# Between two layers: the residual rows requested two blocks ahead, and the low parts of the normed rows moved from GpSimd to VectorE

## The chip, the cores and the metric

The kernel runs on one core of a Trainium2 chip. A core has TensorE (PE in the profile; its weight loads are a row of their own, PEld), VectorE (DVE), ScalarE (ACT), GpSimd (POOL) and SyncE (SP), which issues almost all DMAs here. The metric is the device time of one execution in microseconds; lower is better. Three runs of the kernel before took 1369.54, 1370.9 and 1371.71 us.

## The reference, cut to what matters

The reference is one inference step of a two-layer encoder: 512 prompt rows and 32 sample rows of width 1024. Each layer is `x + (branch * silu(gate)) @ w_out`, with the branch made from `rmsnorm(x) @ w_in`. Layer 0 mixes tokens by RWKV-7, layer 1 by differential attention; both also attend to 256 memory rows, whose keys and values are `rmsnorm(mem) @ w_mem_k` and `@ w_mem_v`. The part at issue is where layer 0 ends and layer 1 begins:

```
x1  = x + out @ w_out[0]                       # residual add of layer 0
h   = x1 * rsqrt(mean(x1*x1) + EPS) * norm_w[1]
mk, mv = rmsnorm(mem) @ w_mem_k[1], rmsnorm(mem) @ w_mem_v[1]
p   = h @ df_in                                # input projection of layer 1
```

## The kernel before, in words

All activations are held transposed: 1024 features are eight tiles of 128 partitions (`KT = 8`), and the 544 tokens (512 + 32) lie along the free axis. Every float32 product is made of three products of rounded numbers. An operand is split into a high part, rounded to fp32r, and a low part, the rest, so `w @ x` is `whi*xh + whi*xl + wlo*xh`. For weights, `raw` arrives by DMA, ScalarE casts it to `whi`, VectorE subtracts to get `wlo` (helper `split`, two halves of 128x512 each). For activations the pair is called `hi`/`lo` in layer 0's output projection, `hh`/`hl` as the normed input of a layer, and `mmh`/`mml` for the memory rows.

One helper records every instruction of TensorE, VectorE, ScalarE and SyncE, so the profile gives them all line 106, and they are told apart by tile names. Up to the end of the output projection the order of each engine's instructions is written out by hand (`self.ordered = True`). After `self.ordered = False` (line 1745) the recording layer chooses the order on each engine by itself. Whatever the source, an engine or a DMA queue works its instructions off in order: one that waits holds all behind it. A DMA on SP also waits until the DMA eight before it (roughly: the one that used the same of eight completion counters) has landed.

The stages around the change, in order of time:

- *The last head pair of layer 0 and the start of its output projection.* The 16 gated outputs lie in a scratch tensor in HBM, `oscr`. Five are fetched and split ahead; the other eleven are fetched in `w_out` (SP: `lo<-oscr`, 272 KB each; then ScalarE `hi<-lo`, VectorE `lo<-lo,hi`).
- *The output projection* `w_out(0, ...)`, with eight output blocks k of 128 features. For each block, `residual` turns the 32x32 pieces of the residual rows `xr` to feature-major on VectorE (`x<-xr`, a stream transpose of 128x544), and `consume` adds TensorE's sums to them and squares them on ScalarE (`sqn`) for the norm (`sums`).
- *`rows(k)`* asks for the residual rows of block k: four DMAs of 64 KB from `x_prompt`, in pieces of 32 numbers, and four of 4 KB from `x_sample`. It is called once ahead (`rows(0)`, line 1717, before `w_out` asks for anything), and then for block k+1 from `residual` of block k.
- *Between the layers* (line 1747 on): the mean of squares by small products (`ps_n`), a reciprocal root of eight small VectorE instructions (`tm_...`), five diagonal tiles `dg` by which TensorE spreads the roots over the partitions (`ps_r`), and the loop over k, lines 1757 to 1764: `hn` (VectorE, 128x512 and 128x32), `hh` (ScalarE cast), `hl = hn - hh` (GpSimd, line 1763). TensorE meanwhile makes the memory keys and values of layer 1 (`mem_kv`: eight blocks of 24 products of 256 columns, `ps_g<-mmh,...`; `memx`, `memz`, `memt` and `ps_mkt` carry its results out), and then starts layer 1's projection with `ps_g<-hh,whi`, `ps_g<-hl,whi`, `ps_g<-hh,wlo`.

The constants are `HNB = 3` (buffers of `hn`) and `RAWS = 5` (buffers of raw weights).

Of the kernel before, what the change touches and what calls it, by code (L numbers as in the profile page):

```python
# [9 lines left out]
F32 = mybir.dt.float32  # L10
# [4 lines left out]
ALU = mybir.AluOpType  # L15
AX = mybir.AxisListType

P = 128
# [4 lines left out]
T = TP + TS  # L23
# [16 lines left out]
HNB = 3  # L40
# [68 lines left out]
class Trunk:  # L109
# [1330 lines left out]
    def layer0(self, mem):  # L1440
        nc, o = self.nc, self.o
# [5 lines left out]
        with ExitStack() as ctx:  # L1447
# [23 lines left out]
            def go(kind, pr):  # L1471

                if kind == "rsq":
                    self.rsqrt(self.r20[:], self.q20[:], self.rk0, "nt")
                elif 0 <= pr < NPAIR:
                    if kind in ("inv", "back", "at"):
                        {"inv": self.rw_invert, "back": self.rw_back, "at": self.rw_at}[kind](sts[pr])
                        return
                    if (kind, pr) not in run:
                        it = run[kind, pr] = self.rw_prep(sts[pr], rkv[pr]) if kind == "prep" else make[kind](sts[pr])  # L1480
                        next(it)
                    next(run[kind, pr], None)
# [203 lines left out]
        with ExitStack() as ctx:  # L1686
            p = self.pool("wo0", 1, ctx=ctx)
            sums = p.tile([P, T], F32, name="sums")
            xs, again = [], self.mem_again(mh, ml)

            def rows(k):

                if k < KT:
                    x = p.tile([P, T], F32, tag="xr", name="xr", bufs=2)
                    for a in range(4):
                        r, f = slice(TS * a, TS * a + TS), slice(k * P + TS * a, k * P + TS * a + TS)
                        self.se.dma_start(x[r, :TP].rearrange("i (b c) -> i b c", c=TS),
                                          self.a["x_prompt"][0, :, f].rearrange("(b i) c -> i b c", i=TS))
                    for a in range(4):
                        r, f = slice(TS * a, TS * a + TS), slice(k * P + TS * a, k * P + TS * a + TS)  # L1700
                        self.se.dma_start(x[r, TP:], self.a["x_sample"][0, :, f])
                    xs.append(x)

            def residual(k, vs):

                if vs[0].start == 0:
                    rows(k + 1)
                    self.ve.transpose(self.x1[:, k, :], xs[k][:])

            def consume(k, ps, v):  # L1710
                x = self.x1[:, k, v]
                self.ve.tensor_tensor(x, ps, x, ALU.add)
                self.square_sums((k, x, v), p, sums)
                if k > 1:
                    next(again, None)

            rows(0)
            self.ahead = after[2:] + [(self.a[n][1], h * P) for n in ("w_mem_k", "w_mem_v") for h in range(MH)] + self.blocks1()
            wout, ahead = self.w_out(0, p, OUT_ORDER, consume, residual, made)

            def both():
                yield from main
                for _ in range(2):
                    self.early.append(self.load(*self.ahead.pop(0)))
                self.until(self.last_split)
                yield from wout
            both = both()

            def fill2(n):
                for i in range(n):  # L1730
                    next(both, None)
                    if i % 6 == 5:
                        self.some(LATER)

            for kind, n in TAIL:
                if kind == "split":
                    ahead(1)
                else:
                    go(kind, NPAIR - 1)
                fill2(n)  # L1740
            for _ in both:
                pass
            while self.later:
                self.later.pop(0)[0]()
            self.ordered = False

            rs = self.token_rms((sums,), p)
            kv = chain(*(self.mem_kv(1, mh, ml, kind, self.psm, "m") for kind in range(2)))
            next(kv)
            pr = [self.psc.tile([P, 512], F32, tag="c", name="ps_r") for _ in range(2)]  # L1750
            for i in range(5):
                n = P if i < 4 else TS
                dg = p.tile([P, P], F32, tag="dg", name="dg", bufs=2)
                self.ve.tensor_scalar(dg[:], self.ident[:], rs[:, i : i + 1], None, ALU.mult)
                c = i % 4 * P
                self.te.matmul(pr[i // 4][:, c : c + n], self.ones[:], dg[:, P - n :], start=True, stop=True)
            for k in range(KT):
                h = p.tile([P, T], F32, tag="hn", name="hn", bufs=HNB)
                for q, c, n in ((0, 0, TP), (1, TP, TS)):
                    self.ve.scalar_tensor_tensor(h[:, c : c + n], self.x1[:, k, c : c + n], self.nw[1][:, k : k + 1],  # L1760
                                                   pr[q][:, :n], ALU.mult, ALU.mult)
                self.ae.copy(self.hh[:, k, :], h[:])
                nc.gpsimd.tensor_tensor(self.hl[:, k, :], h[:], self.hh[:, k, :].bitcast(F32), ALU.subtract)  # L1763
                next(kv, None)
            for _ in kv:
                pass
# [479 lines left out]
```

## Time and profile before

| what | value |
|---|---|
| runs | 1369.54, 1370.9, 1371.71 us |
| the profiled execution | 1371.42 us |
| its span, first to last instruction | 1369.2 us |
| TensorE busy in the span | 1339.3 us (98%), weight loads 1283.9 us (94%) |
| VectorE, ScalarE, GpSimd busy | 939.7, 822.6, 381.9 us |
| granted TensorE clock, mean | 0.998 |

Numbers of a trace are microseconds from the start of the span. A row of a timeline gives start, length, engine, line, operation, tiles, count, and in brackets how long the engine stood idle before it and what ended that. A length of several instructions is from the start of the first to the end of the last; neighbours overlap by a little, since the next starts before the last one's results are all written. Because TensorE carries the span almost alone, the places where its weight loads stand still are what a change can win or lose.

### The profile page before, as it was taken

What the parts mean: (1) busy time and instruction counts of PE and PEld (TensorE: products, weight loads), DVE (VectorE), ACT (ScalarE), POOL (GpSimd) and SP (SyncE); (2) the same over time, 40 slices, a digit from 0 to 9 for tenths busy, and PEclk for the clock granted to TensorE, in tenths of its full rate; (3) what the DMA queues carried; (4) which work ended last, traced back from release to release, by engine and by line L of the source; (5) the groups of instructions that cost most, each with busy time, mean ns of one, the idle gap of its engine ahead of it and who ended that gap; (6) DMA issues with size and microseconds to landing.
All of it is one profiled execution on the core that took longest, in us unless ns stands there. A gap on an engine that the chain in (4) does not pass through costs nothing. (4 is left out here: it accounts for less than half of the span.)

```text
span 1369.2 us, 31861 instructions
## 1 busy us (share of the span) xinstructions
PE 1339.3 (98%) x11845; PEld 1283.9 (94%) x11845; DVE 939.7 (69%) x2353; ACT 822.6 (60%) x2288; POOL 381.9 (28%) x841
## 2 busy tenths in 40 slices
PE   8999999999999999999999999999999999999997
PEld 6988899999999998988999989999999999999997
DVE  5776788888888888667744667775567747667443
ACT  5766777877778777656433466654566537665222
POOL 2138667766686667600000120000000001002000
PEclk9999999999999999999999999999999999999999
DMA  7452322333323332432555563332333323332322
GB/s 224 146 140 70 77 71 57 94 86 74 88 67 84 88 88 64 142 87 76 173 142 147 148 184 88 100 102 82 101 95 94 90 82 94 97 97 79 93 78 73
DMA packets 276964, 139.06 MB, mean 102 GB/s; under 512 B 75769, under 2 KB 265730, under 8 KB 276810
## 3 DMA queue, kind: packets, MB, share of 16 engines
q1 hardware_dynamic: 276746, 137.01, 36.0%
q8 instruction: 94, 1.54, 0.5%
q14 instruction: 60, 0.49, 0.1%
q10 hardware_dynamic: 64, 0.02, 0.0%
HBM read 110.72 MB, written 22.91 MB: 98 GB/s over the span
## 5 line engine op out<-in xcount | busy, mean ns | idle before, releaser
L106 PE MATMUL ps_g<-hh,whi 128*128 128x272 f32 x1808 | 539.7, 299 | 1.0 <-DVE ats L106 0.7
L106 PE MATMUL ps_g<-hh,wlo 128*128 128x272 f32 x1808 | 534.8, 297 | 1.6 <-DVE wlo L106 1.5
L106 PE MATMUL ps_g<-hl,whi 128*128 128x272 f32 x1808 | 532.4, 295 | 0.6 <-DVE hl L106 0.3
L106 PEld LDWEIGHTS ps_g<-hh,whi 128*128 128x128 f32 x1808 | 341.2, 189 | 5.1 <-DVE ats L106 0.9
L106 PEld LDWEIGHTS ps_g<-hh,wlo 128*128 128x128 f32 x1808 | 340.6, 189 | 4.7 <-DVE wlo L106 2.5
L106 PEld LDWEIGHTS ps_g<-hl,whi 128*128 128x128 f32 x1808 | 341.1, 189 | 2.8 <-DVE hl L106 1.3
L106 DVE TENSOR_TENSOR wlo<-raw,whi 128x512 fp32r<-128x512 f32 x314 | 220.1, 712 | 118.3 <-ACT whi L106 114.7
L106 ACT CAST whi<-raw 128x512 fp32r<-128x512 f32 x314 | 188.9, 619 | 115.8 <-PE ps_g L106 62.4
L868 POOL TENSOR_TENSOR tm<-u,m 102x84 f32<-102x84 f32 (+23 forms) x341 | 147.8, 433 | 115.4 <-DMA m<-sc 69.5
L870 POOL TENSOR_TENSOR u<-u,tm 102x84 f32<-102x84 f32 (+23 forms) x341 | 151.6, 445 | 26.6
L106 PE MATMUL ps_g<-hi,wlo 128*128 128x272 f32 x512 | 147.8, 289 | 1.2 <-DVE wlo L106 1.2
L106 PE MATMUL ps_g<-hi,whi 128*128 128x272 f32 x512 | 147.7, 289 | 0.0
L106 PE MATMUL ps_g<-lo,whi 128*128 128x272 f32 x512 | 147.4, 288 | 0.0
L1339 POOL TENSOR_TENSOR lo<-og,hi 128x544 fp32r<-128x544 f32 x8 | 13.2, 1649 | 357.7 <-ACT hi L106 357.2
L106 PEld LDWEIGHTS ps_g<-hi,wlo 128*128 128x128 f32 x512 | 96.4, 188 | 1.7 <-DVE wlo L106 1.6
L106 PEld LDWEIGHTS ps_g<-hi,whi 128*128 128x128 f32 x512 | 96.5, 189 | 0.0
L106 PEld LDWEIGHTS ps_g<-lo,whi 128*128 128x128 f32 x512 | 96.4, 188 | 0.0
L106 ACT ACTIVATE pt<-ps_s,snm 128x128 f32<-128x128 f32 (+3 forms) x96 | 51.0, 532 | 41.7 <-DVE snm L106 41.6
L1763 POOL TENSOR_TENSOR hl<-hn,hh 128x544 fp32r<-128x544 f32 x8 | 12.2, 1536 | 211.4 <-ACT hh L106 211.3
L106 DVE SCALAR_TENSOR_TENSOR SB<-ps_c,dl,sd 64x64 f32<-64x64 f32 x168 | 47.4, 282 | 26.4 <-PE ps_c L106 21.2
L106 ACT COPY sv<-ps_c 64x64 f32<-64x64 f32 x192 | 39.6, 206 | 32.7 <-PE ps_c L106 30.8
L106 ACT ACTIVATE sg<-ps_g 128x272 f32<-128x272 f32 x64 | 25.2, 394 | 41.0 <-PE ps_g L106 38.3
(400 smaller groups left out, 2564.4 us busy)
## 6 DMA issues: line engine op xcount, KB each, us to landing
raw<-in_rw_in_dram SPq DMA_DIRECT2D x114, 256.0 KB
raw<-in_df_in_dram SPq DMA_DIRECT2D x112, 256.0 KB
raw<-in_w_out_dram SPq DMA_DIRECT2D x64, 256.0 KB
oscr<-sg SPq DMA_DIRECT2D x16, 272.0 KB
lo<-oscr SPq DMA_DIRECT2D x16, 272.0 KB
m<-sc SPq DMA_DIRECT2D x33, 128.0 KB
raw<-in_w_mem_v_dram SPq DMA_DIRECT2D x16, 256.0 KB
kh<-kh SPq DMA_DIRECT2D x24, 136.0 KB
```

The costliest lines, as they stand in the source:

```text
L106: return lambda *a, **k: self.trunk.tie(self, issue(*a, **k))
L868: nc.gpsimd.tensor_tensor(tm[:, :n, :wd], u3[:, :n, kx : kx + 1].to_broadcast(sh), m3[:, kx : kx + 1, kx + 1 :].to_broadcast(sh), ALU.mult)
L870: nc.gpsimd.tensor_tensor(u3[:, :n, kx + 1 :], u3[:, :n, kx + 1 :], tm[:, :n, :wd], ALU.add)
L1339: (self.nc.gpsimd if g % 2 and self.o1 else self.ve).tensor_tensor(lo[:], t, hi[:].bitcast(F32), ALU.subtract)
L1763: nc.gpsimd.tensor_tensor(self.hl[:, k, :], h[:], self.hh[:, k, :].bitcast(F32), ALU.subtract)
```

## The change

The residual rows take buffers under the tag `hn` instead of their own two, so rows and normed rows share three buffers. The rows of block k+2 instead of k+1 are asked for in block k, with `rows(0)` and `rows(1)` both called ahead. The subtraction `hl` goes from GpSimd to VectorE.

```diff
-                    x = p.tile([P, T], F32, tag="xr", name="xr", bufs=2)
+                    x = p.tile([P, T], F32, tag="hn", name="xr", bufs=HNB)
...
                 if vs[0].start == 0:
-                    rows(k + 1)
+                    rows(k + 2)
                     self.ve.transpose(self.x1[:, k, :], xs[k][:])
...
             rows(0)
+            rows(1)
...
                 self.ae.copy(self.hh[:, k, :], h[:])
-                nc.gpsimd.tensor_tensor(self.hl[:, k, :], h[:], self.hh[:, k, :].bitcast(F32), ALU.subtract)
+                self.ve.tensor_tensor(self.hl[:, k, :], h[:], self.hh[:, k, :].bitcast(F32), ALU.subtract)
```

What this does to the order of instructions shows at three places. The first is SP's queue where layer 0's output projection begins; `xr` are residual rows, `lo5` to `lo8` gated outputs, `raw` weights. Before:

```order
L106 DMA oscr1_476<-sg2_83 128x544
L106 DMA xr_10584<-in_x_prompt_dram 32x16x32 x4
L106 DMA xr_10584<-in_x_sample_dram 32x32 x4
L106 DMA lo5_10594<-oscr0_475 128x544
L106 DMA lo6_10597<-oscr0_475 128x544
```

Now, from the same place on:

```order
L106 DMA xr_10584<-in_x_prompt_dram 32x16x32 x4
L106 DMA xr_10584<-in_x_sample_dram 32x32 x4
L106 DMA xr_10593<-in_x_prompt_dram 32x16x32 x4
L106 DMA xr_10593<-in_x_sample_dram 32x32 x4
L106 DMA lo5_10603<-oscr0_475 128x544
L106 DMA lo6_10606<-oscr0_475 128x544
```

Eight more DMAs, the rows of block 1, stand ahead of all eleven fetches of gated outputs and of the weights behind them. The last group of eight, which stood between the first weights of `w_mem_k`, is gone from there.

The second place is VectorE at the end of the output projection, where the sums of squares (`sums`) are finished and the root (`tm_m`) begins; `wlo` are low parts of the memory weights:

```order
 L106 TENSOR_TENSOR x_10579<-ps_g,x_10579 128x272
-L106 TENSOR_TENSOR wlo<-raw,whi 128x512
-L106 TENSOR_TENSOR sums<-sums,sqn 128x272
-L106 TENSOR_TENSOR wlo<-raw,whi 128x512
+L106 TENSOR_TENSOR sums<-sums,sqn 128x272
 L106 TENSOR_SCALAR tm_m_11850<-ps_n 128x5
+L106 TENSOR_TENSOR wlo<-raw,whi 128x512
```

The sums now come straight after the last residual add, ahead of both `wlo`. ScalarE's last `sqn` has likewise moved ahead of three `whi`.

The third is VectorE in the loop over k; eight rows of before, from the second `hn` on:

```order
L106 SCALAR_TENSOR_TENSOR hn<-x_10579,PB,ps_r 128x512
L106 SCALAR_TENSOR_TENSOR hn<-x_10579,PB,ps_r 128x32
L106 TENSOR_TENSOR wlo<-raw,whi 128x512
L106 SCALAR_TENSOR_TENSOR hn<-x_10579,PB,ps_r 128x512
L106 SCALAR_TENSOR_TENSOR hn<-x_10579,PB,ps_r 128x32
L106 TENSOR_TENSOR wlo<-raw,whi 128x512
L106 TENSOR_TENSOR memz<-memx,mo 128x256
L106 TENSOR_TENSOR wlo<-raw,whi 128x512
```

Now:

```order
L106 SCALAR_TENSOR_TENSOR hn<-x_10579,PB,ps_r 128x512
L106 SCALAR_TENSOR_TENSOR hn<-x_10579,PB,ps_r 128x32
L106 TENSOR_TENSOR hl<-hn,hh 128x544
L106 TENSOR_TENSOR wlo<-raw,whi 128x512
L106 TENSOR_TENSOR hl<-hn,hh 128x544
L106 TENSOR_TENSOR wlo<-raw,whi 128x512
L106 TENSOR_TENSOR memz<-memx,mo 128x256
L106 SCALAR_TENSOR_TENSOR hn<-x_10579,PB,ps_r 128x512
```

The eight `hl` are spread between the `wlo` and `hn` of VectorE's queue, each waiting for ScalarE's `hh` of the same k. The last `hl` stands behind all eight `hn` and ahead of the `wlo` of layer 1's third weight block.

## The prediction

> **What bounds the kernel now.** I read the page first, then the waits of the weight loads in two stretches, then the queues that those waits point to.
>
> ```profile
> PE 1339.3 (98%) x11845; PEld 1283.9 (94%) x11845; DVE 939.7 (69%) x2353; ACT 822.6 (60%) x2288; POOL 381.9 (28%) x841
> PE 42%; DVE 1%; ACT 0%; issue 0%; DVEq 0%; ACTq 0%
> L1763 POOL TENSOR_TENSOR hl<-hn,hh 128x544 fp32r<-128x544 f32 x8 | 12.2, 1536 | 211.4 <-ACT hh L106 211.3
> ```
>
> TensorE carries the span and the last chain. So only places count where its weight loads stand still. From the fetch of the outputs to the last residual add (664 to 764) the waits of PEld are one row:
>
> ```profile
> PEld ps_g L106 <- DVE wlo L106: 1.0, 1, 1.0
> ```
>
> Between the layers (764 to 800) they are five:
>
> ```profile
> PEld ps_g L106 <- DVE wlo L106: 2.2, 3, 1.2
> PEld ps_mkt L106 <- ACT memx L106: 1.5, 4, 0.6
> PEld ps_r L106 <- DVE dg L106: 0.6, 2, 0.4
> PEld ps_n L106 <- DVE sums L106: 0.4, 1, 0.4
> PEld ps_g L106 <- ACT whi L106: 0.3, 1, 0.3
> ```
>
> They add to 5.0 us: that is all the change can win there. In the first stretch it can win at most 1.0, and lose.
>
> **The change part by part: the rows two blocks ahead.** What was late? The transposes of VectorE are the only readers of `xr`; their group shows the idle time ahead of them in the last column:
>
> ```profile
> L106 DVE STREAM_TRANSPOSE x<-xr 128x544 f32<-128x544 f32 x8 | 5.9, 738 | 0.0
> ```
>
> It is 0.0 for all eight: no row was ever waited for, so asking earlier wins 0. The group of eight DMAs taken from the end of the projection frees SP of 4 us there, also for 0, since PEld waits for nothing between its one wait at 681.6 and 764. The third buffer costs 0 too: by the time `hn` takes it, its rows have been transposed.
>
> The price is at the start. SP's queue before:
>
> ```profile
> 663.36 2.08 SPq L106 DMA_DIRECT2D xr<-in_x_prompt_dram  x4
> 665.49 1.88 SPq L106 DMA_DIRECT2D xr<-in_x_sample_dram  x4
> 667.47 1.79 SPq L106 DMA_DIRECT2D lo<-oscr  x4
> 669.36 3.21 SPq L106 DMA_DIRECT2D raw<-in_w_out_dram  x4
> 672.62 3.34 SPq L106 DMA_DIRECT2D lo<-oscr  x5
> ...
> 684.46 3.41 SPq L106 DMA_DIRECT2D xr<-in_x_prompt_dram  x4
> 687.91 3.35 SPq L106 DMA_DIRECT2D xr<-in_x_sample_dram  x4
> ```
>
> Eight row DMAs take 667.47 - 663.36 = 4.1 us of SP. A second group now stands between the first and `lo`, so the `lo` start at about 671.6. Who waits for them is seen on ScalarE:
>
> ```profile
> 672.06 2.79 ACT L106 CAST hi<-lo 128x544 fp32r<-128x544 f32 x4 [2.77 <-DMA lo<-oscr]
> 678.20 0.65 ACT L106 CAST hi<-lo 128x544 fp32r<-128x544 f32 x1 [3.34 <-DMA lo<-oscr]
> 679.09 0.65 ACT L106 CAST hi<-lo 128x544 fp32r<-128x544 f32 x1 [0.24 <-DMA lo<-oscr]
> 679.64 1.14 ACT L106 CAST whi<-raw 128x512 fp32r<-128x512 f32 x2
> ```
>
> and on the weight loads:
>
> ```profile
> 681.59 0.19 PEld L106 LDWEIGHTS ps_g<-hi,wlo 128*128 128x128 f32 x1 [0.98 <-DVE wlo L106]
> ```
>
> The `whi` at 679.64 is queued behind casts that waited for `lo9` and `lo10`; its `wlo` is what TensorE waited 0.98 us for. That chain has no slack: what delays `lo10` delays TensorE as much. Does `lo10` come 4.1 us later? The windows:
>
> ```profile
> core 0: us, PE busy (x) PEld busy (x) DVE busy (x) ACT busy (x) POOL busy (x), PEclk, DMA share, GB/s
> 664.00:668.00 4.00, 4.00 (x34) 4.00 (x33) 3.61 (x9) 1.27 (x3) 0.00 (x0) 1.00 0.61 122
> 669.00:679.00 10.00, 10.00 (x82) 9.91 (x81) 6.18 (x12) 3.53 (x6) 0.00 (x0) 1.00 0.99 330
> 764.00:800.00 36.00, 33.18 (x260) 30.87 (x259) 29.82 (x56) 21.00 (x49) 13.30 (x12) 1.00 0.54 157
> ```
>
> From 669 to 679 the DMA engines are busy 0.99 of the time: nine `lo` and four `raw` are moved as fast as they go, so the train shifts as a whole, by the 4.1 us. TensorE stalls in two bites of the same shift (first at `lo5`, used about 1.6 us after it was ready, so 4.1 - 1.6 = 2.5; the rest at the `wlo`). Nothing later gives it back: all behind it follows TensorE. Bounds: 0 at the low end, if the casts had slack that I do not see (their 2.77 and 3.34 us of waiting speak against that); at the high end 3.41 + 3.35 = 6.8 us, what the same eight DMAs took at 684.46. I take 4.1, the nearer row: same place in the queue, same neighbours. **Term 1: +4.1 us.**
>
> The Trainium skill, "DMA: Bandwidth & Descriptors", in the table of measured transfers under Bandwidth, gives 0.95 us of DMA time for 64 KB and 0.68 us for 4 KB (measured from GpSimd's queue). By that a group of rows is 4 x 0.95 + 4 x 0.68 = 6.5 us, an estimate, and the sum would be 2.4 us higher. The trace does not agree: from 664 to 668, while SP issued rows, the DMA engines were busy only 0.61 of the time, so issue set the pace and not transfer.
>
> **The low parts on VectorE.** While GpSimd works on `hl`, VectorE's subtractions stretch. In the window 779.5 to 799 of its groups (after the bar: busy us, mean ns of one, idle time ahead):
>
> ```profile
> L106 DVE TENSOR_TENSOR wlo<-raw,whi 128x512 fp32r<-128x512 f32 x10 | 11.5, 1176 | 1.2 <-ACT whi L106 1.2
> L106 DVE TENSOR_TENSOR memz<-memx,mo 128x256 f32<-128x256 f32 x2 | 2.6, 1287 | 0.0
> ```
>
> and from 764 to 779.5, with GpSimd idle:
>
> ```profile
> L106 DVE TENSOR_TENSOR wlo<-raw,whi 128x512 fp32r<-128x512 f32 x7 | 4.7, 689 | 3.9 <-ACT whi L106 3.9
> L106 DVE TENSOR_TENSOR memz<-memx,mo 128x256 f32<-128x256 f32 x2 | 0.8, 421 | 0.0
> ```
>
> The stretch is 10 x (1.176 - 0.689) + 2 x (1.287 - 0.421) = 4.9 + 1.7 = 6.6 us of VectorE, all in the stage where PEld waits for `wlo`. It goes. What comes is eight subtractions of 128x544; such instructions stand in the trace:
>
> ```profile
> 682.05 1.35 DVE L106 TENSOR_TENSOR lo<-lo,hi 128x544 fp32r<-128x544 f32 x2
> 683.33 1.28 DVE L106 TENSOR_TENSOR wlo<-raw,whi 128x512 fp32r<-128x512 f32 x2
> ...
> 772.33 0.17 DVE L106 TENSOR_SCALAR tm_m<-ps_n 128x5 f32<-128x5 f32 x1 [0.32 <-PE ps_n L106]
> ...
> 777.90 1.72 DVE L106 SCALAR_TENSOR_TENSOR hn<-x,PB,ps_r 128x512 f32<-128x512 f32 x4
> 779.53 0.68 DVE L106 TENSOR_TENSOR wlo<-raw,whi 128x512 fp32r<-128x512 f32 x1
> ```
>
> Two `lo` take 683.33 - 682.05 = 1.28 us, 0.64 each, so eight `hl` 5.1 us: VectorE's load falls by 1.5 us. But now they wait in line. I laid the new order out with these lengths. The sums stand ahead of two `wlo`, so `tm_m` starts at about 769.9 instead of 772.3, and the first `hn` at about 775.7 instead of 777.9. From there to the last `hl` VectorE has 8 `hn` pairs of (779.53 - 777.90) / 2 = 0.82, 8 `hl` of 0.64, 12 `wlo` of 0.62 and 3 `memz` of 0.35: 6.5 + 5.1 + 7.4 + 1.1 = 20.1 us, so 795.8, and 1.0 for waits on ScalarE's `hh`: about 796.8. GpSimd ended its last at 797.48 + 1.35 = 798.8:
>
> ```profile
> 797.48 1.35 POOL L1763 TENSOR_TENSOR hl<-hn,hh 128x544 fp32r<-128x544 f32 x1 [1.01 <-ACT hh L106]
> ```
>
> TensorE's waits then: for `wlo` 2.2 to 0 and for `whi` 0.3 to 0 (made in time without the stretch), for `sums` 0.4 to 0, for `memx` 1.5 to 0.3 (ScalarE's copies no longer bunch behind late `hh`), for `dg` 0.6 to 0.9 (TensorE arrives earlier), and new, for the last `hh` and `hl`, 1.1, since without the other stalls it reaches them at 795.7. That is 2.3 against 5.0. **Term 2: -2.7 us.** Bounds: -5.0, all waits gone; and +1, if the queue ends its last `hl` a microsecond after GpSimd did. I take what the layout gives, nearer to the first, since VectorE's load falls. GpSimd's two sets of clears for layer 1, which came after its last `hl`, now run some 35 us earlier and are waited for by nobody.
>
> **Sum.** +4.1 - 2.7 = +1.4 us on the profiled execution of 1371.4 (span 1369.2 and 2.2 around it), which lies 0.5 above the median of the three runs, 1370.9. Against that median: 1372.3 us, +0.1%, below the 0.2% (2.7 us) that a measurement of this kernel tells from no change.
>
> **The rivals.**
> - *Slower: VectorE's queue becomes the new wait.* One `hl` whose `hh` is late holds the `wlo` and `hn` behind it, and TensorE waits for `wlo` as before. Decides from where the last `hl` ends after 798.8, so with 2 us more of waits than I laid out. Then term 2 is 0, and the time 1370.9 + 4.1 = 1375.0. For it: ScalarE casts `whi` in the same queue. Against: 6.6 us of stretch go. Chance 0.16.
> - *Slower: the second rows cost the 6.8 us of 684.46:* 1370.9 + 6.8 - 2.7 = 1375.0. For it: pieces of 32 numbers are slow to move. Against: the share of 0.61. Chance 0.05.
> - *Faster: the `lo` train is hidden.* If the casts' wait were shortened elsewhere, term 1 is under 1 and the time near 1370.9 - 2.7 = 1368.2. Against: 0.99 of DMA share and the 0.98 us stall. Chance 0.12.
> - *All 5.0 us between the layers go*, term 1 holds: 1370.0; no difference that can be told. That lies inside the forecast's case, as does the part of the change that does nothing, the rows that nobody waited for.
>
> **How the numbers follow.** Forecast 0.67 (1369 to 1373.6), the slower rivals 0.21, the faster 0.12. With the edges, where a forecast in its own range can cross the bound: faster 0.13, same 0.64, slower 0.23. The range for 8 in 10 goes from the faster rival's 1368.2 to the slower ones' 1375.0, each widened by 0.5, by which the profiled execution and the median differ: 1367.7 to 1375.5.
>
> **What would show it.** In the profile after: sixteen `xr` DMAs on SP ahead of `lo`, `lo` at about 671.6, the first `hi` cast at about 676; PEld waiting about 5 us instead of 1.0 between 664 and 764, for `lo`, `hi` or `wlo`; `wlo` at 0.69 us throughout; `hl` on VectorE ending 2 us sooner relative to the last residual add than before; PEld's waits between the layers near 2.3. Wrong would be: no new wait near 675 to 686 (term 1), or waits for `wlo` and `hl` between the layers still above 4 (term 2).

## The result: 0.18% slower

| kernel | median | runs | ratio to before, 95% interval |
|---|---|---|---|
| before | 1370.65 us | 22 (1369.14 to 1372.45) | |
| changed | 1373.41 us | 22 (1371.47 to 1374.77) | 1.0018 (1.0012 to 1.0025) |

The change costs 2.8 us by the medians and 0.18% by the ratio, which is a figure of its own and not the quotient of the medians: clear of zero, and at the edge of the 0.2% (2.7 us) that the forecast called no change. The forecast was 1372.3 us. The profiled execution has a span of 1371.5 us, 2.3 more than before:

```profile
span 1371.5 us, 31837 instructions
PE 1340.3 (98%) x11845; PEld 1285.4 (94%) x11845; DVE 937.7 (68%) x2361; ACT 822.1 (60%) x2288; POOL 368.1 (27%) x833
```

Both traces hold 11,845 weight loads, and outside the stretch from 765 to 803, where TensorE's order changed too, they come in the same order. So the start of the n-th load in one can be set against the start of the n-th in the other. That lateness, the measure used from here on, is 0.0 us at 660, +5.8 at 700 and 764, +2.1 at 812, and +2.4 near the end. So the gated outputs' stretch lost 5.8 us, and the stage between the layers won 3.7 back; the rest adds 0.3.

**The loss.** The queue of SP after, from its first row DMA on:

```profile
663.35 2.08 SPq L106 DMA_DIRECT2D xr<-in_x_prompt_dram  x4
665.47 1.88 SPq L106 DMA_DIRECT2D xr<-in_x_sample_dram  x4
667.39 2.02 SPq L106 DMA_DIRECT2D xr<-in_x_prompt_dram  x4
669.45 2.41 SPq L106 DMA_DIRECT2D xr<-in_x_sample_dram  x4
671.96 1.79 SPq L106 DMA_DIRECT2D lo<-oscr  x4
```

The first `lo` is asked for at 671.96, where it was 667.47. The waits of the weight loads from 664 to 764, one row of 1.0 us before, are now:

```profile
PEld ps_g L106 <- ACT whi L106: 1.9, 1, 1.9
PEld ps_g L106 <- DVE lo L106: 1.1, 2, 0.6
PEld ps_g L106 <- DVE wlo L106: 1.1, 1, 1.1
PEld ps_g L106 <- ACT hi L106: 1.1, 2, 0.7
```

They add to 5.2 us, 4.2 more than before. The lateness grew by 5.8. The missing 1.6 us stands in the windows just ahead of and behind 685.7, in the column after the busy times (PEclk):

```profile
682.30:685.70 3.40, 1.16 (x8) 0.73 (x6) 2.25 (x4) 2.88 (x6) 0.00 (x0) 1.00 0.52 188
685.70:689.10 3.40, 3.00 (x13) 3.00 (x14) 3.40 (x7) 2.25 (x5) 0.00 (x0) 0.50 0.93 276
```

TensorE worked for 1.16 of 3.40 us, and then the granted clock was 0.50 for the next 3.4 us: 13 products where the same stretch of before held 30. At half clock, 3.4 us of work lose 1.7.

**The gain.** From 764 to 812 the waits were 5.0 us before; after they are 1.7:

```profile
PEld ps_mkt L106 <- ACT memx L106: 0.7, 2, 0.6
PEld ps_g L106 <- ACT hh L106: 0.7, 1, 0.7
PEld ps_r L106 <- DVE dg L106: 0.3, 1, 0.3
```

VectorE's subtractions from 779.5 to 803 (after the bar: busy us, mean ns of one) are back at the length that they had with GpSimd idle, 685 ns instead of 1176, and `hl` costs 717 ns each, 5.7 us for the eight:

```profile
L106 DVE TENSOR_TENSOR wlo<-raw,whi 128x512 fp32r<-128x512 f32 x14 | 9.4, 685 | 0.4 <-ACT whi L106 0.2
L106 DVE TENSOR_TENSOR hl<-hn,hh 128x544 fp32r<-128x544 f32 x8 | 5.7, 717 | 1.2 <-ACT hh L106 1.2
```

### The profile page after: what moved, and what is told of

The parts are those of the page before. It is cut to its first block, busy times and chain, and to the rows that moved or that the text cites. A ratio compares the mean times of both kernels' runs of the same rounds, so it can differ in the third digit from the quotient of the medians.

```text
span 1371.5 us, 31837 instructions
## 1 busy us (share of the span) xinstructions
PE 1340.3 (98%) x11845; PEld 1285.4 (94%) x11845; DVE 937.7 (68%) x2361; ACT 822.1 (60%) x2288; POOL 368.1 (27%) x833
## 4 chain that ended last, share of the span: by engine, by line
PE 87%; ACT 4%; DVE 4%; DMA 2%; issue 1%; SPq 1%; POOL 1%; DVEq 0%; ACTq 0%; POOLq 0%
PE ps_g L106 61%; PE ps_c L106 6%; PE ps_s L106 2%; PE ps_o L106 2%; PE ps_at L106 2%; PE ps_v L106 2%; PE ps_mm L106 1%; SPq L106 1%; PE ps_w L106 1%; PE ps_mo L106 1%; PE ps_aT L106 1%; PE ps_yc L106 1%; PE ps_wa L106 1%; PE ps_kv L106 1%; PE ps_q L106 1%
## 5 line engine op out<-in xcount | busy, mean ns | idle before, releaser
L106 DVE TENSOR_TENSOR wlo<-raw,whi 128x512 fp32r<-128x512 f32 x314 | 215.5, 696 | 114.9 <-ACT whi L106 111.3
```

The source lines that it names most:

```text
L106: return lambda *a, **k: self.trunk.tie(self, issue(*a, **k))
```

## The experiments

Each kernel's median stands beside that of the kernel before in the same set of runs; before itself moved between the sets, so kernels of different sets are compared by their ratios. For the order at the seam alone the medians and the ratio do not even agree in sign: there the runs show no difference. The last three columns are changes of TensorE's lateness in the profiled execution: in the gated outputs' stretch (660 to 700), between the layers (764 to 812), and over the whole from 660 to the end. They are of one execution each. The six kernels whose first stretch has no rows added ahead and none taken away show -0.2 to +0.5 there, and the seven with rows two ahead, low parts on VectorE and GpSimd not subtracting show -3.4 to -3.9 between the layers; a difference between two rows as small as that says nothing by itself.

| kernel | median, before | ratio, 95% interval | 660-700 | 764-812 | total |
|---|---|---|---|---|---|
| changed | 1373.41, 1370.65 | 1.0018 (1.0012 to 1.0025) | +5.8 | -3.7 | +2.4 |
| rows part alone | 1376.91, 1371.67 | 1.0035 (1.0023 to 1.0048) | +7.8 | -1.6 | +6.1 |
| low parts alone | 1369.49, 1371.67 | 0.9985 (0.9976 to 0.9994) | +0.2 | -2.7 | -2.0 |
| both, second rows late | 1367.93, 1371.67 | 0.9974 (0.9963 to 0.9985) | 0.0 | -3.8 | -3.5 |
| low parts, first rows late | 1368.22, 1371.67 | 0.9977 (0.9967 to 0.9987) | +0.1 | -2.8 | -2.6 |
| both, half of the second rows ahead | 1372.66, 1371.39 | 1.0007 (0.9998 to 1.0016) | +4.7 | -3.6 | +1.4 |
| second rows late, GpSimd subtracts too | 1374.37, 1371.39 | 1.0022 (1.0012 to 1.0032) | +0.5 | +2.4 | +2.9 |
| both, three groups ahead | 1376.82, 1371.39 | 1.0041 (1.0027 to 1.0054) | +8.2 | -3.8 | +4.7 |
| order at the seam alone | 1370.84, 1371.39 | 1.0002 (0.9993 to 1.0010) | -0.1 | -1.3 | -1.0 |
| changed, TensorE's wait filled | 1373.46, 1372.01 | 1.0011 (1.0002 to 1.0019) | +4.5 | -3.7 | +1.2 |
| order and low parts | 1368.81, 1372.01 | 0.9976 (0.9965 to 0.9986) | +0.2 | -3.8 | -3.2 |
| second rows late, GpSimd clears | 1368.69, 1372.01 | 0.9975 (0.9965 to 0.9985) | -0.2 | -3.9 | -3.6 |
| both, all rows late | 1367.34, 1372.01 | 0.9967 (0.9955 to 0.9978) | -1.1 | -3.4 | -4.1 |

### The two parts, one at a time

The rows part alone (from the changed kernel):

```diff
-                self.ve.tensor_tensor(self.hl[:, k, :], ...
+                nc.gpsimd.tensor_tensor(self.hl[:, k, :], ...
```

> The row part of the change alone: rows two blocks ahead in the shared buffers, the low parts still on GpSimd. Theory A (the second group of rows ahead of the gated outputs delays TensorE, the stretch of VectorE by GpSimd is untouched): PEld waits between 664 and 764 near 5.2 us as in the changed kernel, TensorE 5.9 us late at 700, wlo between the layers still near 1.18 us, time 1370.65 + 5.9 = 1376.5 us. Rival B (the gain between the layers came with the rows, whose last group of DMAs left the end of the projection): TensorE's waits from 764 to 803 fall from 5.0 to about 1.7 here too, and the time is that of the changed kernel, 1373.4 us. Rival C (the half clock after the wait is the luck of one execution): 1370.65 + 4.2 = 1374.8 us.

The low parts alone (from the kernel before):

```diff
-                nc.gpsimd.tensor_tensor(self.hl[:, k, :], ...
+                self.ve.tensor_tensor(self.hl[:, k, :], ...
```

> The VectorE part of the change alone: the eight low parts on VectorE, rows as before (one block ahead, two buffers of their own). Theory A: no new wait from 664 to 764 (1.0 us), wlo near 0.69 us between the layers, PEld's waits from 764 to 812 about 1.7 us instead of 5.0, time 1370.65 - 3.7 = 1367.0 us. Rival B (that gain came with the rows): about 1370.6 us. Rival D (without the earlier delay, which let the weights and ScalarE get ahead of TensorE, the queue of VectorE is tighter): about half the gain, 1368.8 us.

The rows part alone loses 7.8 us in the first stretch (its waits there are 6.0 us, and its half clock lasted two of the 3.4 us pieces), but it also wins 1.6 us between the layers, though GpSimd still stretches the subtractions:

```profile
L106 DVE TENSOR_TENSOR wlo<-raw,whi 128x512 fp32r<-128x512 f32 x12 | 12.6, 1062 | 1.2 <-ACT whi L106 1.2
```

Up to the end of the output projection this kernel is the changed one; that it lost 7.8 us there and the changed one 5.8 is a difference between two executions, in how long the half clock lasted. The runs (1.0035) lie between theory A (1.0043) and rival C (1.0030), and their interval holds both; rival B (1.0020) lies outside.

The low parts alone win 2.7 us there, not 3.7. So theory A had the first stretch right, and each theory had a part of the second: the gain between the layers has two sources, 1.0 to 1.6 us of it from the rows. Rival D forecast about half the gain, and the size came near it (2.1 us by the ratio), but not for its reason: in the next kernel nothing is delayed earlier, and 3.8 us are won.

### Where in the queue the rows stand

Both parts, with the second group behind the gated outputs:

```diff
             rows(0)
-            rows(1)
...
                 if vs[0].start == 0:
+                    if k == 0:
+                        rows(1)
                     rows(k + 2)
```

> The whole change, but the second group of rows is asked for together with the third in the first block's residual, behind the gated outputs. Theory A: the place in the queue is all that costs, so the same as with the low parts alone, 1367.0 us, and no half clock. Rival E (two groups of rows in a row on the queue at 684 hold the weights behind them for another 4 to 7 us, and TensorE waits there): a new wait for whi or wlo near 695 to 705, 1368 to 1371 us.

The low parts, rows one block ahead, and the first group asked for after gated output 14:

```diff
-            rows(0)
...
                 came.append((g, self.fetch(p, g)))
+                if i == 0 and g == 14:
+                    extra(-1, None)      # residual(-1, ...) calls rows(0)
```

> The low parts on VectorE, rows one block ahead, and the first group of rows asked for behind the gated output 14 instead of ahead of 5: 4.1 us less of the queue ahead of the gated outputs. Theory A (that train has no slack): the wait of 1.0 us at 681.6 goes and nothing more, since TensorE waits for nothing else up to 764: 1366.0 us. Rival F (the train is held by what comes earlier, the write of the gated outputs, so it starts no sooner): 1367.0 us. Rival E (the rows, now at 673 to 680 between large transfers, land late for their transpose at 688, or hold the later gated outputs): a wait for x or hi near 685, 1367 to 1369 us.

With the second group late, the loss in the first stretch is gone (0.0) and the gain of 3.8 stays: 0.26% faster than before, theory A's time, so the place of eight DMAs is the whole loss of the change. Moving the first group as well, with the low parts alone, took away the wait at 681.6 and put one of 1.1 us behind the last gated outputs at 689, as rival E had it in kind; theory A's 1366.0 us (0.9966) lies just outside the interval:

```profile
689.21 0.19 PEld L106 LDWEIGHTS ps_g<-hi,whi 128*128 128x128 f32 x1 [0.49 <-ACT hi L106]
689.97 0.19 PEld L106 LDWEIGHTS ps_g<-lo,whi 128*128 128x128 f32 x1 [0.57 <-DVE lo L106]
```

Both edits together, on the kernel with both parts:

```diff
-            rows(0)
-            rows(1)
...                                          # rows(0) behind gated output 14
+                    if k == 0:
+                        rows(1)
```

> The kernel with the second group of rows late, and the first group behind the gated output 14 as well. Theory A (the wait of 1 us at 681.6 only moves on to the last gated outputs, as it did with the low parts alone): within 0.5 us of the kernel with the rows late, 3.6 us below before. Rival Q (the two gains add): 0.7 to 1 us more, 4.5 us below before.

Here the weight loads wait for nothing from 664 to 764. It is the best version measured: 0.33% below before. The first stretch wins 1.1 us, as rival Q had it; against the kernel with only the second group late it is 0.6 us better over the whole trace and 1.0 by the ratios. The intervals overlap, so the last microsecond is not settled by the runs. Why the wait at 689 stayed away here and not in the other kernel is not shown. Both have the same order on SP up to there, and SP reached the write of the last gated outputs at 679.99 here and at 681.10 there, so it may be no more than a difference between two executions.

How the loss grows with what stands ahead, half of the second group:

```diff
-            rows(1)
+            rows(1, prompt only)     # the sample rows of block 1 come in residual(0)
```

> The changed kernel with only half of the second group of rows (the four DMAs from the prompt) ahead of the gated outputs, its other four behind them. Theory A (the delay is the issue time that stands ahead, 2.1 us for four): PEld's waits from 664 to 764 near 1.0 + 2.1 = 3.1 us instead of 5.2, and by that less idle no stretch at half clock: 2.1 us above the kernel with the group behind (1367.9), 1370.0 us. Rival C (any such wait brings 3.4 us at half clock, which cost 1.7): 1371.7 us. Rival G (the pieces of 4 KB from the sample rows are what holds the queue): no new wait, 1368 us.

And a third group (the first block's `residual` then asks for none):

```diff
             rows(1)
+            rows(2)
```

> The changed kernel with a third group of rows (block 2) ahead of the gated outputs. Theory A (every eight row DMAs shift the whole train by 4.1 us, and TensorE by as much): PEld's waits from 664 to 764 near 9.3 us, the stretch at half clock one or two windows of 3.4 us (1.7 us of loss each, one of them in the changed kernel already): 1373.4 + 4.1 = 1377.5 to 1379.2 us. Rival I (the first 4.1 us filled a hole and further rows are limited by their transfers, of 6 us or more): 1380 us or more. Rival B (the train's start is set elsewhere and the wait stays): 1373.4 us.

Four DMAs more give waits of 3.1 us, as theory A had them (1.0 + 2.1):

```profile
PEld ps_g L106 <- ACT whi L106: 2.0, 1, 2.0
PEld ps_g L106 <- DVE wlo L106: 1.1, 1, 1.1
```

But a half clock followed here too, for 6.8 us, and the loss was 4.7, so rival C is nearest. In these two executions half of the group costs nearly as much as the whole; by the ratios (1.0007 and 1.0018) it costs 1.5 us less. The third group is cheaper than theory A or rival I said: +8.2 in the first stretch instead of 9.9 to 11.6, and by the ratios 3.2 us above the changed kernel instead of 4.1 to 5.8. Its waits are 7.4 us, most of them in one piece,

```profile
681.01 0.29 PEld L106 LDWEIGHTS ps_g<-hi,whi 128*128 128x128 f32 x1 [4.87 <-ACT hi L106]
```

and the half clock (678.7 to 685.5) began while TensorE still stood in that wait. Measured against the lateness at 660, the first cast of `whi` behind the train came 3.8 us later than in the changed kernel (688.90 - 684.01 - 1.1), so the train shifted nearly as before. That the slow clock used up some of the later waiting fits this and is not shown by itself.

### The half clock

In all these traces the pieces of half clock between 600 and 810 are 3.41 us or twice that, and in one trace their starts lie whole multiples of 3.4133 us apart (131.33, 800.35 and 1366.96 in the kernel where GpSimd subtracts too: 196 and 166 of them), as on a grid. Where the clock fell, the weight loads had been busy for 0.7 to 1.4 us of the piece of this grid before; between 600 and 810 no piece at full clock with 1.7 us or more was followed by a fall. To see whether standing still is the cause, 14 products with a zero weight tile were put just where TensorE stood still for 1.95 us (they add zero to sums in progress):

```diff
+                if i == 0 and (k, q) == (0, 1) and gs[0] == half[1][0]:
+                    for n in range(14):
+                        v = halves[n % 2]
+                        self.te.matmul(ps[0][v.start // TH][:, :TH], zero[:], o[half[0][0]][0][:, v], start=False, stop=False)
```

> The changed kernel with 14 products of a zero weight tile added on TensorE (14 x 0.125 = 1.75 us) just where it stood still for 1.95 us, ahead of the second weight block of the output projection; they add zero to sums in progress. Theory L (the loss of 1.7 us beyond the waits is TensorE's own half clock, brought on by standing still): no stretch at half clock near 686, TensorE late by 4.2 instead of 5.9 us at 700, 1.7 us faster than the changed kernel: about 1 us above the kernel before instead of 2.7. Rival M (the half clock has another cause, or the second wait of 1.1 us is enough for it): same as the changed kernel, 2.7 us above before. Rival N (the added products are late themselves): more than 2.7 us above before.

The same two windows in its trace:

```profile
682.30:685.70 3.40, 3.40 (x26) 2.96 (x24) 1.75 (x3) 2.38 (x5) 0.00 (x0) 1.00 0.70 243
685.70:689.10 3.40, 2.50 (x21) 2.50 (x21) 3.40 (x7) 2.64 (x5) 0.00 (x0) 1.00 0.84 232
```

The clock stays at 1.00, and the lateness from 660 to 700 is 4.5 instead of 5.8 us (the loads behind the added ones are counted with 14 taken off). A lucky place of the grid does not explain it: wherever a stretch of 3.41 us is begun between 668 and 700, the loads are busy for at least 1.7 us of it here, while the emptiest in the changed kernel has 0.3. So more work made TensorE earlier: theory L, shown in the trace. In the runs its 1 us above before (1.0007) lies within the interval and rival M's 2.7 (1.0020) just outside, but the interval overlaps that of the changed kernel.

The mean granted clock of all runs points the same way: 0.9969 over the 22 runs of the changed kernel, 0.9980 to 0.9983 over three sets of runs of the kernel before, 0.9976 with the wait filled. The first difference, 0.0011 to 0.0014 of 1371 us, is 3.0 to 3.8 us at half clock in a run on average, about one piece.

The Trainium skill, "TensorE: Matmul & The Clock Gate", Part 1, has a monitor with free-running windows of 3413 ns that gives half the clock after an idle one; the length agrees with the 3.41 us here. Its table of goals asks for no idle gap of TensorE over about 3 us; here shorter ones were enough, one of 2.03 us with half of the rows ahead, and in the changed kernel 1.95 us and the first 0.74 us of the next wait within one piece.

### What the rows won between the layers

In the list of the order, the kernel with only the low parts has ScalarE's last square (`sqn`) behind two casts of memory weights and a copy, and VectorE's last `sums` between two `wlo`, as before; each kernel with rows two ahead has both in front (of two casts, then, and not of three as said ahead of the prediction). There the products of `ps_n`, for which the root waits, stand further forward on TensorE too: the last is its 7201st weight load instead of the 7217th. The root's first instruction, low parts alone:

```profile
773.19 0.17 DVE L106 TENSOR_SCALAR tm_m<-ps_n 128x5 f32<-128x5 f32 x1 [0.32 <-PE ps_n L106]
```

and both parts with the second rows late, whose trace is 0.2 us less late at 764:

```profile
770.62 0.17 DVE L106 TENSOR_SCALAR tm_m<-ps_n 128x5 f32<-128x5 f32 x1 [0.97 <-PE ps_n L106]
```

It is 2.6 us earlier. Was it the order, or SP's free queue? A fence makes the order by itself:

```diff
             queue.last = ins
+        elif self.fence and queue in (self.ae, self.ve):
+            self.order(ins, queue.last)
...
-            self.ordered = False
+            self.ordered, self.fence = False, True
```

> The kernel before with one thing changed: at the seam between the hand-ordered part and the rest, ScalarE's and VectorE's later instructions may not be put ahead of the last hand-ordered ones, so the last sqn and sums come ahead of the memory weights' casts, as they do in the changed kernel. Low parts on GpSimd, rows one block ahead. Theory J (what the rows two ahead won between the layers, 1.6 us, is this order, a by-product of the order being chosen anew): the root (tm_m) starts 2 to 3 us sooner, TensorE's waits from 764 to 812 fall by 1 to 1.6 us, 1369.3 us. Rival K (it is the free queue of SP at the end of the projection): no gain, 1370.7 us.

And the fence with the low parts:

```diff
-                nc.gpsimd.tensor_tensor(self.hl[:, k, :], ...
+                self.ve.tensor_tensor(self.hl[:, k, :], ...
```

> The fence at the seam (last sqn and sums ahead of the memory weights) together with the low parts on VectorE; rows one block ahead as before. Theory J (what the rows two ahead won between the layers was this order): as the kernel with the rows late, 1.5 us better than the low parts alone, 3.6 us below before (1368 us). Rival K (it was the free queue of SP): as the low parts alone, 2.0 us below before (1369.5 us).

The root's first instruction with the fence alone:

```profile
772.12 0.17 DVE L106 TENSOR_SCALAR tm_m<-ps_n 128x5 f32<-128x5 f32 x1 [1.62 <-PE ps_n L106]
```

It stands 0.2 us ahead of before (772.33), and with the low parts at 772.35: theory J's first sign, 2 to 3 us, did not come. The fence moves the sums, but the last product of `ps_n` is TensorE's 7216th weight load, against the 7217th of before. So the fence's order is not the one that the rows brought.

Still the fence alone wins 1.3 us between the layers in the trace, where TensorE's wait for `sums` is gone (the waits that the view lists fall from 5.0 to 4.2); the runs (1.0002, 0.9993 to 1.0010) do not show that gain, and lie above the 1369.3 us that theory J gave. The fence with the low parts, rows one block ahead as before, wins 3.8 us there and stands at 0.9976, level with the kernel that has the rows two ahead (0.9974) and below the low parts alone (0.9985, intervals overlapping). So between the layers the traces bear theory J out in size: another order wins as much without the rows two ahead and without SP's free queue. That the rows won their part by the earlier root, or by nothing but the order, is argued and not shown, and that the fence pays by itself is not shown by the runs.

### What stretches VectorE

To the kernel with the second rows late, GpSimd's subtractions were added again, into a buffer that nobody reads:

```diff
                 self.ve.tensor_tensor(self.hl[:, k, :], h[:], self.hh[:, k, :].bitcast(F32), ALU.subtract)
+                nc.gpsimd.tensor_tensor(junk[:], h[:], self.hh[:, k, :].bitcast(F32), ALU.subtract)
```

> The kernel with the second group of rows late (1367.9 us, low parts on VectorE), and beside it the eight subtractions are made on GpSimd as well, into a buffer that nobody reads; the order on VectorE between the layers is the same to the instruction. Theory A (GpSimd's subtractions stretch VectorE's): wlo near 1.0 to 1.2 us and memz near 1.2 us while GpSimd works, some 7 us more on VectorE's queue, which TensorE can't hide: 4 to 7 us slower, 1372 to 1375 us. Rival H (the stretch of before was one of these tiles' places or of the order, and the gain came from the order): wlo 0.69 us and 1367.9 us.

```profile
L106 DVE TENSOR_TENSOR hl<-hn,hh 128x544 fp32r<-128x544 f32 x6 | 11.3, 1882 | 0.0
L106 DVE TENSOR_TENSOR wlo<-raw,whi 128x512 fp32r<-128x512 f32 x12 | 8.8, 752 | 0.2 <-ACT whi L106 0.2
L106 DVE SCALAR_TENSOR_TENSOR hn<-x,PB,ps_r 128x512 f32<-128x512 f32 x6 | 4.4, 735 | 0.0
```

The loss, 6.2 us between the layers against the kernel without it, is what theory A had (part of it is a half clock of 3.4 us from 800.3 on), but the place is not: the subtraction that meets GpSimd's is now mostly `hl` (1882 ns instead of 717), and `wlo` hardly suffers. The rows of one block show why:

```profile
783.87 1.28 DVE L106 TENSOR_TENSOR wlo<-raw,whi 128x512 fp32r<-128x512 f32 x2
784.80 1.57 POOL L1767 TENSOR_TENSOR junk<-hn,hh 128x544 f32<-128x544 f32 x1 [3.19 <-ACT hh L106]
785.08 1.89 DVE L106 TENSOR_TENSOR hl<-hn,hh 128x544 fp32r<-128x544 f32 x1
```

The second `wlo` was under way when GpSimd began, and kept its length. The `hl` began 0.28 us behind GpSimd and ended 0.59 us after GpSimd's end, 0.58 to 0.59 us in all six blocks: nearly what it takes from its start to the next one's where nothing holds it, 0.63 us (787.91 to 788.54 in the changed kernel). So it is less a slowing than a wait for the other's end, and the place in the order decides which instruction pays.

`hn`, which has one operand in PSUM (`ps_r`), never met GpSimd's subtractions in this trace (but for 58 ns). In the kernel before, one pair ran wholly beside them and kept its length (0.89 us alone), while the `wlo` behind it took 1.80 us:

```profile
779.56 4.98 POOL L1763 TENSOR_TENSOR hl<-hn,hh 128x544 fp32r<-128x544 f32 x3 [204.41 <-ACT hh L106]
780.13 0.90 DVE L106 SCALAR_TENSOR_TENSOR hn<-x,PB,ps_r 128x512 f32<-128x512 f32 x2
781.51 1.80 DVE L106 TENSOR_TENSOR wlo<-raw,whi 128x512 fp32r<-128x512 f32 x1 [0.48 <-ACT whi L106]
```

Then GpSimd with writes alone:

```diff
+                for _ in range(2):
+                    nc.gpsimd.memset(h[:], 0.0)      # with HNB = 4
```

> The kernel with the rows late (3.6 us below before), with four buffers of normed rows instead of three, and after each low part GpSimd clears that block's normed rows twice: it writes and reads nothing. Theory O (GpSimd holds VectorE's subtractions by its reads): wlo 0.69 us and hl 0.72 us, and the time of the kernel with the rows late within 1 us, 1367 to 1369 us. Rival P (any work of GpSimd on this memory holds them): wlo and hl at 1.2 to 1.9 us as with the subtractions on GpSimd, 1371 to 1374 us. By the Trainium skill, SBUF — State Buffer, Who interferes with whom, an instruction of GpSimd that only writes does not contend with a VectorE instruction with two inputs.

```profile
L106 DVE TENSOR_TENSOR wlo<-raw,whi 128x512 fp32r<-128x512 f32 x14 | 9.5, 690 | 3.7 <-ACT whi L106 3.5
L106 DVE TENSOR_TENSOR hl<-hn,hh 128x544 fp32r<-128x544 f32 x8 | 5.8, 721 | 1.1 <-ACT hh L106 1.1
...
L1767 POOL MEMSET hn<- 128x544 f32 x16 | 8.8, 553 | 214.8 <-DMA out_dram<-memt 202.2 <-DVE hl L106 9.5 <-DMA raw<-in_w_mem_v_dram 2.6
```

Sixteen clears of GpSimd, 8.8 us, in the same stage, and no subtraction is longer for it: five `wlo` ran beside a clear for 0.54 us or more and took 689 to 694 ns, as those beside none (683 to 695). That is theory O in its outcome: writes alone do not hold VectorE. That GpSimd's reads do is what is left; no run here has GpSimd read alone. The page of the Trainium skill that the expectation names agrees with these traces: contention for a VectorE instruction with two SBUF inputs, none for one with at most one, none from a GpSimd instruction that only writes.

## Why the prediction was right in sign, and what in it was wrong

- *Rows never waited for, so nothing won by asking earlier:* right. With the second group late the first stretch is 0.0.
- *The group gone from the end of the projection, for 0:* wrong for the rows part as a whole. With the rows two ahead the order around the seam was chosen anew, and the rows alone win 1.6 us there; the fence wins 1.3 by another order, without SP's free time. The prediction saw the sums move and booked them under the low parts.
- *Term 1, +4.1 us:* the mechanism was right: sixteen row DMAs ahead of `lo`, a train with no slack, casts late, TensorE late in two bites. The waits grew by 4.2 us. The bites: 2.2 us for `hi` and `lo` (2.5 forecast) and 3.0 for `whi` and `wlo` (2.6 forecast with the 1.0 of before). The term left out that TensorE then runs at half clock, some 1.6 us more; it measured 5.8.
- *The price of 6.5 us by the table of the Trainium skill, "DMA: Bandwidth & Descriptors", Bandwidth:* the second group took SP 671.96 - 667.39 = 4.6 us, nearer to the 4.1 of the sum, as the share of 0.61 had it.
- *Term 2, -2.7 us:* measured -3.7. The stretch went as worked out, and the root started where the layout had it (775.72, which is 769.9 and 5.8 of lateness). The last `hl` ended 0.9 us sooner after the last residual add than before, not 2. Of the waits, `wlo`, `whi` and `sums` went to 0 as laid out, `dg` to 0.3 (0.9 forecast), `memx` to 0.7 (0.3) and the last `hh` to 0.7 (1.1 with `hl`). The waits alone fell by 3.3; the other 0.4 us is in no wait that the view lists. That the low parts alone win just 2.7 is a coincidence: the layout had the new order in it, which the rows brought.
- *Sum +1.4:* +2.4 in the trace. Two sizes were off, +1.7 and -1.0, and 0.3 us came late in layer 1. That the time still came within 1.1 us of the forecast is partly luck, since the two errors have opposite signs.
- *Rival, VectorE's queue as the new wait:* did not come. It sat idle for 1.2 us ahead of one `hl`, and TensorE's new wait is 0.7 us for `hh`.

## What to carry to other kernels

Ask of each prefetch what it stands in front of: a transfer that nobody waited for, asked for earlier, can only push back those that are waited for, and here the same request 18 us later (685.19 instead of 667.39) was worth 5.8 us in the traces. Take a change apart before judging it: one half of this one was faster by itself. Where a scheduler chooses the order, part of a change's gain may be an order, and a fence of a few lines can show whether such a gain is to be had without the change.

## What the runs showed of the hardware that was not expected

- TensorE's granted clock fell to 0.50 for 3.41 or 6.83 us after a piece of 3.41 us in which the weight loads were busy for 1.4 us or less, though no single wait was longer than 2.0 us in two of the cases. It lasted one such piece in the changed kernel, where TensorE was busy 3.0 us of it, and two with half of the rows ahead, where it was busy 2.6 of the first. 1.75 us of products with zeros in the wait kept the clock at 1.00.
- The half clock also shows at about 131 us, for 3.41 us, in four of the traces (order alone, order and low parts, all rows late, GpSimd subtracting too) and not in the others, at a place that no edit touches:

```profile
131.30:134.70 3.40, 3.40 (x36) 3.06 (x35) 0.81 (x1) 1.45 (x7) 2.85 (x8) 0.51 0.52 140
```

  This row is of the order-alone kernel; in the changed one the same stretch is at 1.00. From 120 to 145 us TensorE lost 0.6 to 0.8 us against before in these four traces and lost nothing in the other nine, so it is one source of the scatter of about 3 us between runs of one kernel. Busy time does not decide it: the weight loads were busy for 2.1 to 2.5 us of the piece before, though with products of tiles of 32x32 for the most part (64 of 78 in the order-alone kernel). What sets the four apart is the grid: counted back in steps of 3.4133 us, a piece begins between 127.4 and 127.9 in each of them, and in none of the other ten. That this decides it was not tried.
